# Placing a matmul stream's operands at the upper end of SBUF: the same program with other addresses

## The chip, the cores and the metric

The kernel runs on one core of one Trainium2 chip. The metric is the device time of one execution in microseconds. The kernel before was timed in three runs.

## What is computed

The reference is two transformer blocks of two layers each, on one sequence of 512 tokens with 1,024 features, all in float32. Cut to what matters here:

```python
# block 1, per layer l
h = rmsnorm(x, n1[l]) * (1 + sc1) + sh1           # sc1, sh1, g1, ... = silu(c) @ w_ada[l] + b_ada[l]
x = x + g1 * token_mixers(h, w_in[l], ...)        # conv, dilated attention, gated scan, then @ w_out[l]
h = rmsnorm(x, n2[l]) * (1 + sc2) + sh2
x = x + g2 * conv_ffn(h, w_up[l], w_down[l])      # 22 gated pairs of 128 channels
# block 2, per layer l
u = rmsnorm(x, g[l]) * (1 + scale) + shift
z = u @ w_in_2[l]                                 # three attention branches and their gates
x = x + gate * (merged(z, w_br_*) @ w_out_2[l])
```

Nearly all arithmetic is in products of a 1,024 by N weight matrix with the activations, features on partitions and tokens along the free dimension.

## The kernel before

**The weight stream.** Every weight matrix is cut into chunks of 128 output columns. A chunk is one `Slot` (line 117), and `run` (line 813) goes through the slots in order. For a slot, `w_load` brings the float32 chunk into a tile `raw` (128 by 1,024, three buffers), `w_hi` casts it to float32r in `hi`, and `w_lo` writes the remainder raw - hi to `lo` (three buffers each). The activations are held in the same form: `hh` and `hl` are the two float32r parts of the normed input, 128 partitions by 8 tiles by 512 tokens. `k_step` (line 804) then makes three matmuls per tile of 128 features, all into one PSUM bank:

```python
self.mm(p[:, c], wh, hh, start, False, cost)      # hi^T hh
self.mm(p[:, c], wh, hl, False, False, cost)      # hi^T hl
self.mm(p[:, c], wl, hh, False, stop, cost)       # lo^T hh
```

The weight part is the stationary operand, loaded before each matmul, and the activation part is the moving operand of 512 columns. At the end of a layer's half, `turn_over` (line 864) works in halves of 256 tokens, so that one half's norm runs beside the other half's products.

**Where operands lie.** Three kinds of tiles serve as operands of these products. The moving operand is `hh`/`hl`, or a piece of the arena `mx` (8 units of 512 float32r) or of the arena `rar` (24 units in the feed-forward phase, 8 in block 2), where the mixers' and the gates' results are split by `split_to`. The stationary operand is `hi`/`lo`, but in `turn_over` it can also lie in `mx` (slots marked `lead`), in `hh`/`hl` (`in_h`, line 2160) or in `rar` (`place`, line 2142).

All SBUF tiles come out of tile pools that are laid one after another from the lower end: `cst` (among others `x`, `hh`, `hl`, `mx` and the float32 arena `stay`, in this order), `ring` (`raw`, `hi`, `lo`), `adar` (`ada`), `sm`, and last a pool `work` that each phase opens anew in `phase` (line 650), with the float32 `arena`, then `rar`, then for block 2 the tables `cos` and `sin`. From the tiles' sizes, in bytes of a partition: `x` lies at 23,648, `hh` at 40,032, `hl` at 56,416, `mx` at 72,800, `stay` at 89,184, `raw` at 113,312, `hi` at 125,600, `lo` at 137,888 (to 150,176), `ada` at 150,176, `arena` from 159,136, `rar` from 175,520 in the feed-forward phase (to 224,672) and from 208,288 in block 2. The last byte used is 228,768.

**The order of the work.** The program is written out by hand: the order of each engine's instructions is fixed when the kernel is built. A planner emits stages of streams (attention, scan, norms) between the matmuls of the slots, by estimated times (`charge`, `pe`, `begin`, `keys`). Its estimates go by a tile's name and the offset inside it, not by an address. VectorE and ScalarE instructions are issued through `Timed` (line 113 in the profile), matmuls through `mm` (line 344) and transposes through `tp` (line 348); DMAs of the stream are issued on the SP queue in `load` (line 410).

Of the kernel before, what the change touches and what calls it, by code (L numbers as in the profile page):

```python
# [10 lines left out]
F32R = mybir.dt.float32r  # L11
# [6 lines left out]
P = 128  # L18
# [10 lines left out]
MIX = (0, 1, 2, 3, 4, 5, 6, 7)  # the order in which w_out takes the tiles of the mixers' results  # L29
FIRST = 4  # L30
U = 512  # one arena unit: 512 float32 per partition
# [23 lines left out]
# microseconds from the end of one engine's instruction to the start of another's that waits for it  # L55
# [3 lines left out]
# columns of the packed per-feature vectors  # L59
# [32 lines left out]
def sub(t, off, dims):  # L92
    """A view of t's partitions with its own free pattern, off elements in."""
    return bass.AP(tensor=t.tensor, offset=t.offset + off, ap=[list(t.ap[0])] + [list(d) for d in dims])


def chunked(buf):
    """A unit as [P, 4, P]."""
    return buf.ap.rearrange("p (c d) -> p c d", c=4)


class Timed:
    """An engine whose instructions also advance an estimate of when its queue is through."""
# [13 lines left out]
class Slot:  # L117
    """One product of the weight stream: psum (+)= chunk^T rhs; with parts several, of (tiles of the chunk, consume)."""
# [10 lines left out]
class Arena:  # L129
    """Memory in units. Single units come out of the smallest gaps, there the longest free one."""  # L130
# [32 lines left out]
class Arenas:  # L163
    """Working memory: a part that stays and one that a phase has."""
# [28 lines left out]
class Kernel:  # L193
    PD = 4  # weight loads this many slots ahead
    PS = 2  # splits this many slots ahead
    ARENA = 50

    def __init__(self, ctx, tc, ins, out, cfg):
# [8 lines left out]
        self.cst = pool("cst", 1)  # L207
        self.ring = pool("ring", 3)
# [20 lines left out]
    def keys(self, ap):  # L229
        """The pieces of memory an access pattern touches, as the estimate tracks them."""  # L230
        name = ap.tensor.name
        if name in self.alias:
            return (self.alias[name],)
        d = ap.ap
        lo = ap.offset % d[0][0]
        neg = sum(min(0, st * (n - 1)) for st, n in d[1:])
        pos = sum(max(0, st * (n - 1)) for st, n in d[1:])
        return [(name, u) for u in range((lo + neg) // KU, (lo + pos) // KU + 1)]

    def begin(self, eng, reads, writes):  # L240
        """When an instruction of eng may start, by what it reads and writes."""
# [73 lines left out]
    def banks(self, tag, n=2):  # L315
        """A stream's psum tiles, once those before them there are estimated to be through. Until their results
        are read, the stream must not yield."""
# [9 lines left out]
    def turned(self, pool, shape, dt, tag, bufs):  # L327
        """The next tile of a tag."""
# [34 lines left out]
    def copy(self, out, in_, scale=1.0, bias=BAL):  # L363
        """A copy on the engine that is estimated to be through with it first."""
# [45 lines left out]
    def load(self, out, src, q=None):  # L410
        """A DMA, on the SP queue unless q says another."""
# [13 lines left out]
    def drain(self, *names):  # L425
        """Emit stages until the streams of these names (none: all) are done."""
# [28 lines left out]
    def lock(self, name, n=1, room=0):  # L455
        """At most n at once; another one only with this much room."""
# [15 lines left out]
    def get(self, k=1, reserve=0):  # L472
        """Buffer for the weight stream's own results; keeps room that lets the streams go on."""
# [15 lines left out]
    def setup(self):  # L489
# [7 lines left out]
        self.hh = ct("hh", [P, KT, S], F32R)  # L497
        self.hl = ct("hl", [P, KT, S], F32R)
        self.phase_stack = self.phase_key = None
        self.mx = Arena(ct("mx", [P, 8 * U], F32R), 8)  # L500
# [26 lines left out]
    def cond(self, b):  # L527
        """silu(c) of block b on all partitions."""
# [9 lines left out]
    def start_up(self):  # L538
        """The first modulations, the input with its sums of squares and the first products, in the order in
        which DMA brings their data in."""  # L540
        b, l = self.cfg[0]
        duo = self.slots[:FIRST]
        # brings the array's clock up before the first data are in
# [106 lines left out]
    def phase(self, n, nr, rope=False):  # L650
        """New working memory: n units of float32 and nr of float32r."""
# [10 lines left out]
        self.rar = Arena(pool.tile([P, nr * U], F32R, name=self.nm("rar")), nr) if nr else None  # L662
# [5 lines left out]
    def load_consts(self):  # L668
        """A stream: the constants that are not needed at once."""
# [15 lines left out]
    def lower_bounds(self):  # L685
        """lb[l] = cumsum(p)[l] - p[0], p the softmax of lb_gamma over the layers."""
# [37 lines left out]
    def ada_until(self, b, l, t0, n):  # L724
        """The modulations t0..t0+n-1 are in and have their bias."""
# [13 lines left out]
    def w_hi(self, j):  # L739
        """The upper part of slot j's chunk, if there is room for it."""  # L740
# [8 lines left out]
        elif len(self.split) < RING:  # L749
            self.split.append(s)  # L750
            s.hi, s.lo = (self.turned(self.ring, [P, KT * P], F32R, t, RING) for t in ("hi", "lo"))
        else:
            return False
# [8 lines left out]
    def through(self, s):  # L762
        """Slot s's products are out."""
# [12 lines left out]
    def whole(self, j):  # L776
        """Whether slot j works on its chunk as it is."""
# [15 lines left out]
    def ahead(self, upto):  # L793
        """One more split, in two steps."""
# [4 lines left out]
    def until_k(self, s, p, kt, c=ALL):  # L799
        """When the products of k_step could start."""  # L800
# [41 lines left out]
    def products(self, s, c, half, *consume_at):  # L842
        """Emits a slot's products for the tokens c, with stages of the streams between them."""
# [20 lines left out]
    def turn_over(self, i, k):  # L864
        """The last k slots before a norm and the first ones after it, in halves of the tokens: one half's norm
        goes on during the other half's products."""
# [13 lines left out]
        # brings in the table of Sqrt ahead of its use  # L880
# [53 lines left out]
    def stay_get(self):  # L934
        """A unit that the change of phase leaves alone."""
# [6 lines left out]
    def go(self):  # L942
        """The next stage of a stream, whenever it comes."""
# [9 lines left out]
    def bias_mm(self, bb, duo, kt, only=None):  # L953
        """W^T B of the tile kt."""
# [5 lines left out]
    def scaled(self, accs):  # L960
        """The products of after_norm times the tokens' 1/rms."""
# [7 lines left out]
    def norm_done(self, duo, ts, bb, dve=False):  # L969
        """Shifts the scaled products of after_norm and hands them on."""  # L970
# [27 lines left out]
    def norm1_of(self, b, l):  # L998
        """Where block b's layer l has its first norm's scale, shift and weight."""
        return b, l, 8, 0, f"n1_{l}" if b == 0 else f"ng_{l}"  # L1000

    def norm_prep(self, b, l, sc, sh, w, fin):
        """Before a norm: A = weight (1 + scale), with the last norm's weight of block 1 where both follow each
        other (fin)."""
# [9 lines left out]
    def stat_tile(self, n, c=ALL):  # L1014
        """Adds the squares of x's tile n (tokens c), those of the one before it once these are on their way."""
# [16 lines left out]
    def h_raw(self, n):  # L1032
        """x's tile n times A."""
# [4 lines left out]
    def rms_rows(self, st, n, scale):  # L1038
        """1/sqrt(st*scale + eps) of st's n columns, tokens on partitions."""
# [5 lines left out]
    def norm_stream(self):  # L1045
        """rb: 1/rms of the tokens, on all partitions, from the sums of squares; with fin that of both norms,
        and rb1 that of the first."""
# [31 lines left out]
    def half_norm(self, hf, c, outs, me, after):  # L1079
        """A stream: the norm of the tokens c, as norm_stream and h_tile; with outs the last one and its result."""  # L1080
# [49 lines left out]
    def fin_stream(self):  # L1130
        """x becomes block 1's result: the last norm's weight and scale."""
# [5 lines left out]
    def h_tile(self, n, bufs, n1, n0=0):  # L1137
        """The first part of tile n and the second of tile n-1."""
# [14 lines left out]
    def v_tokens(self, vT, box):  # L1153
        """A stream: vT [feature, token] to V [token, chunk, feature]."""
# [8 lines left out]
    def two(self, outs, lhsT, rhs, start, stop, n, k0=0):  # L1163
        """The same product of n columns for both heads, side by side in the array."""
# [3 lines left out]
    def pv_add(self, pv, V, j, o, n, rhs, start, stop):  # L1168
        """pv[:, o:o+n] of both heads += V's chunk j times rhs, one operand per head."""
# [3 lines left out]
    def attend(self, heads, span, stride, size, score, V, vo, tag, done, extra=0):  # L1173
        """A stream: pv += V^T P^T of two heads, P made by score from q k^T. span(qt): the keys of query tile qt,
        from which chunk on and how many; P^T's block (kt, qt) lies at kt * stride + qt * P; score adds to the
        products itself where it takes extra units of memory."""
# [59 lines left out]
    def softmax(self, m, sc, bias, cap, nmx, rs):  # L1236
        """m = exp(sc + bias - max), of two heads; nmx: minus the maximum (that of cap too), rs: the sums."""
# [11 lines left out]
    def conv_taps(self, l, a, acc):  # L1249
        """The taps of both channel tiles, one at a time."""  # L1250
# [85 lines left out]
    def scan_stream(self, l, p, q, T0b, Kb, vbox, gbox, out):  # L1336
        """Both directions of the gated scan of heads 2p and 2p+1, by levels of sibling blocks."""
# [11 lines left out]
        def scores(w, lhsT, rhs, cost):  # L1349
            """Per chunk and block of w keys: its scores with the w queries of rhs(chunk, block), on the keys'  # L1350
            partitions."""
# [9 lines left out]
        # the scores within blocks of 32, [key, head, chunk, query of the key's block]  # L1361
# [56 lines left out]
        # between the chunks: the state after a chunk, sum over its tokens of k (decayed to its end) v  # L1418
# [72 lines left out]
    def block1_layer(self, l):  # L1491
        """Adds the layer's slots."""
# [15 lines left out]
        def give(kt):  # L1508
            """A mixer's result, to its place in w_out's order: split at once, but for the second half, which
            goes where h is until the last product with h is emitted."""  # L1510
# [808 lines left out]
```

## Time and profile before

| what | us |
|---|---|
| median of 3 runs (lowest, highest) | 2616.85 (2615.37, 2617.15) |
| span of the profiled execution, first to last instruction | 2612.9 |
| PE busy | 2567.3 (98%) |
| PEld busy (weight loads, beside PE) | 1990.7 (76%) |
| DVE busy | 1774.0 (68%) |
| ACT busy | 1339.9 (51%) |
| mean granted TensorE clock | 0.997 |

PE is the matrix engine, PEld its weight loads, DVE is VectorE, ACT ScalarE. The page's busy time of PE is a union: matmuls are pipelined and overlap one another, so a matmul's own duration is longer than the distance to the next one. What a matmul costs in a dense stream is that distance, start to start, which is read from the timeline. A row of the groups' view gives line, engine, operation, the names out<-in, partitions and columns of the array, the shape, the count, busy time and mean duration in ns, and the idle time before it.

### The profile page before, as it was taken

To read this page: it belongs to the slowest core of one execution; us is meant where nothing else is said; L and a number is where in the kernel's file an instruction comes from. 1 tells how busy PE (TensorE), PEld (TensorE's weight loads), DVE (VectorE), ACT (ScalarE), POOL (GpSimd) and SP (SyncE) were. 2 spreads that over 40 slices of the span, in tenths; PEclk is the share of its full clock that TensorE was granted. 3 is DMA by queue.
4 is the path that set the end of the run, shared out by engine and by line. 5 is a ranking of instruction groups with operands and counts; after the bars stand their busy time and mean duration, and the time that the engine had idled before them with its cause. 6 is when DMAs were issued, how large, how long until landed. Compare 5 with 4: busy or idle time off the path is not lost.

```text
span 2612.9 us, 39181 instructions
## 1 busy us (share of the span) xinstructions
PE 2567.3 (98%) x15404; PEld 1990.7 (76%) x15404; DVE 1774.0 (68%) x3368; ACT 1339.9 (51%) x2345; POOL 0.2 (0%) x4
## 2 busy tenths in 40 slices
PE   9999999999999999999999999999999999999998
PEld 5767788888977678888887677777779667777787
DVE  7898676655589767665667896556556697546645
ACT  4686553323457664342345446666435455666622
POOL 0000000000000000000000000000000000000000
PEclk9999999999999999999999999999999999999999
DMA  7433333444333232343442222223332122222222
GB/s 260 137 136 115 119 113 137 145 145 144 114 136 112 89 113 82 129 144 129 129 137 81 73 81 94 100 93 102 108 126 96 57 69 77 89 77 89 85 89 89
DMA packets 90071, 290.32 MB, mean 111 GB/s; under 512 B 10016, under 2 KB 13728, under 8 KB 89888
## 3 DMA queue, kind: packets, MB, share of 16 engines
q1 hardware_dynamic: 87728, 281.76, 31.8%
q10 hardware_dynamic: 2160, 6.06, 0.7%
q8 instruction: 122, 2.00, 0.3%
q14 instruction: 61, 0.50, 0.1%
HBM read 285.69 MB, written 2.10 MB: 110 GB/s over the span
## 4 chain that ended last, share of the span: by engine, by line
PE 85%; DVE 9%; ACT 4%; issue 1%; DMA 1%; SPq 0%; ACTq 0%; DVEq 0%
PE proj L344 70%; PE sc L344 7%; DVE arena L113 5%; PE tr L348 3%; PE pva L344 3%; ACT arena L113 2%; PE pvs L344 1%; DVE lo L113 1%; DVE sm L113 1%; ACT L113 1%; PE tr L344 1%; DVE hl L113 1%; ACT hi L113 0%; DMA arena<-w_in 0%; DMA raw<-w_in 0%
## 5 line engine op out<-in xcount | busy, mean ns | idle before, releaser
L344 PE MATMUL proj<-hh,hi 128*128 128x512 f32 (+1 forms) x2232 | 905.8, 406 | 5.7 <-ACT arena L113 3.1
L344 PE MATMUL proj<-hl,hi 128*128 128x512 f32 (+1 forms) x2232 | 879.5, 394 | 5.1 <-DVE hl L113 5.1
L344 PE MATMUL proj<-hh,lo 128*128 128x512 f32 (+1 forms) x2232 | 879.1, 394 | 0.5 <-DVE lo L113 0.5
L344 PEld LDWEIGHTS proj<-hh,hi 128*128 128x128 f32 x2232 | 419.7, 188 | 144.8 <-issue 42.5
L113 DVE TENSOR_TENSOR lo<-raw,hi 128x1024 fp32r<-128x1024 f32 (+2 forms) x381 | 436.2, 1145 | 100.8 <-ACT hi L113 95.8
L344 PEld LDWEIGHTS proj<-hh,lo 128*128 128x128 f32 x2232 | 419.8, 188 | 100.4 <-DVE lo L113 1.0
L344 PEld LDWEIGHTS proj<-hl,hi 128*128 128x128 f32 x2232 | 420.4, 188 | 95.7 <-DVE hl L113 8.3
L113 ACT CAST hi<-raw 128x1024 fp32r<-128x1024 f32 (+2 forms) x340 | 333.9, 983 | 102.9 <-PE proj L344 65.0
L344 PE MATMUL proj<-rar,hi 128*128 128x512 f32 x672 | 209.6, 393 | 0.0
L113 DVE SCALAR_TENSOR_TENSOR arena<-proj,colt,arena 128x511 f32<-128x511 f32 x164 | 122.9, 749 | 116.7 <-ACT arena L113 113.8
L113 DVE TENSOR_TENSOR arena<-arena 128x512 f32<-128x512 f32 (+8 forms) x321 | 173.0, 558 | 23.9 <-ACT arena L113 16.9
L113 ACT ACT_TABLE_LOAD x134 | 171.9, 1283 | 17.6 <-DVE sm L113 8.6
L113 ACT COPY arena<-tr 128x512 f32<-128x512 f32 (+3 forms) x266 | 111.0, 458 | 118.3 <-PE tr L348 108.2
L113 DVE SCALAR_TENSOR_TENSOR ada<-ada,cbc 128x1024 f32<-128x1024 f32 x128 | 155.8, 1217 | 0.2 <-DMA ada<-ada 0.2
L113 ACT ACTIVATE arena<-proj,colt 128x512 f32<-128x512 f32 x82 | 56.4, 688 | 184.5 <-PE proj L344 182.3
L113 ACT ACTIVATE arena<-proj 128x512 f32<-128x512 f32 x113 | 66.8, 599 | 160.2 <-PE proj L344 152.6
L344 PEld LDWEIGHTS proj<-rar,hi 128*128 128x128 f32 x672 | 124.8, 188 | 30.8 <-issue 4.6
L344 PE MATMUL sc<-arena 64*32 64x32 f32 (+6 forms) x3024 | 143.6, 248 | 3.1 <-issue 2.6
L344 PE MATMUL proj<-mx,hi 128*128 128x512 f32 x432 | 138.0, 400 | 2.4 <-DVE x L113 2.4
L113 DVE SCALAR_TENSOR_TENSOR x<-proj,mod,x 128x512 f32<-128x512 f32 (+1 forms) x102 | 64.6, 634 | 106.5 <-PE proj L344 105.7
L113 ACT ACTIVATE arena<-arena,sm 128x512 f32<-128x512 f32 (+3 forms) x180 | 105.2, 585 | 59.9 <-DVE sm L113 58.8
L344 PE MATMUL proj<-rar,lo 128*128 128x512 f32 x336 | 130.9, 390 | 0.0
(219 smaller groups left out, 3073.8 us busy)
## 6 DMA issues: line engine op xcount, KB each, us to landing
raw<-w_in SPq DMA_DIRECT2D x190, 512.0 KB, 3.3
ada<-ada SPq DMA_DIRECT2D x128, 512.0 KB, 4.5
raw<-w_up SPq DMA_DIRECT2D x88, 512.0 KB, 3.3
raw<-w_out SPq DMA_DIRECT2D x32, 512.0 KB, 3.4
raw<-w_down SPq DMA_DIRECT2D x32, 512.0 KB, 3.5
raw<-w_br SPq DMA_DIRECT2D x48, 256.0 KB, 2.7
arena<-ada SPq DMA_DIRECT2D x16, 512.0 KB, 7.3
raw<-w_down SPq DMA_DIRECT2D x16, 384.0 KB, 3.2
```

The costliest lines, as they stand in the source:

```text
L113: return f(*a, **kw)
L344: self.nc.tensor.matmul(out, lhsT, rhs, start=start, stop=stop)
L348: self.nc.tensor.transpose(out, in_, self.ident)
```

## The change

No instruction is added, removed or reordered. Tiles get other places. `hh`, `hl` and `mx` move from `cst` to a new pool `opd`, `hi` and `lo` from `ring` to a new pool `halves`, and each phase's `rar` from `work` to a pool `high` of its own. These three pools are laid on the right side, that is downwards from the upper end. What is left (`cst`, `ring` with `raw` alone, `adar`, `sm`, `work`) closes up at the lower end. The rest of the diff removes comments.

```diff
         self.cst = pool("cst", 1)
+        self.opd = pool("opd", 1, side="right")
+        self.halves = pool("halves", 3, side="right")
         self.ring = pool("ring", 3)
...
-        self.hh = ct("hh", [P, KT, S], F32R)
-        self.hl = ct("hl", [P, KT, S], F32R)
+        self.hh = self.opd.tile([P, KT, S], F32R, name="hh")
+        self.hl = self.opd.tile([P, KT, S], F32R, name="hl")
...
-        self.mx = Arena(ct("mx", [P, 8 * U], F32R), 8)
+        self.mx = Arena(self.opd.tile([P, 8 * U], F32R, name="mx"), 8)
...
-        self.rar = Arena(pool.tile([P, nr * U], F32R, name=self.nm("rar")), nr) if nr else None
+        self.rar = None
+        if nr:
+            high = self.phase_stack.enter_context(self.tc.tile_pool(name=self.nm("high"), bufs=1, side="right"))
+            self.rar = Arena(high.tile([P, nr * U], F32R, name=self.nm("rar")), nr)
...
-            s.hi, s.lo = (self.turned(self.ring, [P, KT * P], F32R, t, RING) for t in ("hi", "lo"))
+            s.hi, s.lo = (self.turned(self.halves, [P, KT * P], F32R, t, RING) for t in ("hi", "lo"))
```

## Rows read from the trace of the kernel before

**Rows 1.** The page's first part: span, busy time by engine.

```profile
span 2612.9 us, 39181 instructions
...
PE 2567.3 (98%) x15404; PEld 1990.7 (76%) x15404; DVE 1774.0 (68%) x3368; ACT 1339.9 (51%) x2345; POOL 0.2 (0%) x4
```

**Rows 2.** The chain that ended last: shares of the span by engine and line.

```profile
PE 85%; DVE 9%; ACT 4%; issue 1%; DMA 1%; SPq 0%; ACTq 0%; DVEq 0%
PE proj L344 70%; PE sc L344 7%; DVE arena L113 5%; PE tr L348 3%; PE pva L344 3%; ACT arena L113 2%; PE pvs L344 1%; DVE lo L113 1%; DVE sm L113 1%; ACT L113 1%; PE tr L344 1%; DVE hl L113 1%; ACT hi L113 0%; DMA arena<-w_in 0%; DMA raw<-w_in 0%
```

**Rows 3.** Stretches: length, PE, PEld, DVE, ACT, POOL busy, PE clock, DMA.

```profile
1050.00:1300.00 250.00, 250.00 (x1076) 201.69 (x1076) 155.38 (x199) 91.25 (x121) 0.00 (x0) 1.00 0.40 134
...
100.00:250.00 150.00, 144.18 (x1727) 103.58 (x1725) 132.72 (x277) 111.33 (x201) 0.00 (x0) 1.00 0.36 125
...
1450.00:1550.00 100.00, 95.73 (x472) 68.64 (x471) 90.68 (x187) 51.66 (x105) 0.00 (x0) 1.00 0.19 64
```

**Rows 4.** Groups by shape, PE: the stream's matmuls of 512 columns.

```profile
L344 PE MATMUL proj<-hh,hi 128*128 128x512 f32 x2200 | 896.6, 408 | 3.6 <-ACT arena L113 3.1 <-ACT hh L113 0.5
L344 PE MATMUL proj<-hl,hi 128*128 128x512 f32 x2200 | 870.6, 396 | 5.1 <-DVE hl L113 5.1
L344 PE MATMUL proj<-hh,lo 128*128 128x512 f32 x2200 | 870.2, 396 | 0.5 <-DVE lo L113 0.5
...
L344 PE MATMUL proj<-rar,hi 128*128 128x512 f32 x672 | 209.6, 393 | 0.0
...
L344 PE MATMUL proj<-mx,hi 128*128 128x512 f32 x432 | 138.0, 400 | 2.4 <-DVE x L113 2.4
L344 PE MATMUL proj<-rar,lo 128*128 128x512 f32 x336 | 130.9, 390 | 0.0
...
L344 PE MATMUL proj<-mx,lo 128*128 128x512 f32 x216 | 85.3, 395 | 0.0
```

**Rows 5.** Timeline of PE, 672.3 to 677.4 us: start, duration, what.

```profile
672.46 0.62 PE L344 MATMUL proj<-rar,hi 128*128 128x512 f32 x2
...
675.18 0.63 PE L344 MATMUL proj<-mx,hi 128*128 128x512 f32 x2
...
676.58 0.40 PE L344 MATMUL proj<-rar,hh 128*128 128x256 f32 x2
```

**Rows 6.** Timeline of PE, 313 to 317.6 us: half slots of 256 columns.

```profile
314.26 0.28 PE L344 MATMUL proj<-hl,hi 128*128 128x256 f32 x1
...
316.87 0.28 PE L344 MATMUL proj<-hh 128*128 128x256 f32 x1
...
317.59 0.28 PE L344 MATMUL proj<-hh 128*128 128x256 f32 x1
```

**Rows 7.** Groups by shape, PE: matmuls of 256 columns, by where the weights lie.

```profile
L344 PE MATMUL sc<-hh,mx 128*128 128x256 f32 x224 | 53.6, 284 | 0.0
...
L344 PE MATMUL proj<-hl,rar 128*128 128x256 f32 x64 | 17.7, 277 | 0.0
...
L344 PE MATMUL proj<-mx,hl 128*128 128x256 f32 x16 | 4.5, 284 | 0.0
```

**Rows 8.** Groups by shape, DVE: one operation on high and on low tiles.

```profile
L113 DVE TENSOR_TENSOR arena<-arena 128x512 f32<-128x512 f32 x159 | 109.2, 688 | 9.7 <-ACT arena L113 6.0 <-PE sc L344 2.1
...
L113 DVE TENSOR_TENSOR sq<-sq,arena 128x512 f32<-128x512 f32 x32 | 21.5, 684 | 0.1
```

**Rows 9.** Groups by shape, ACT: one operation into high and into low tiles.

```profile
L113 ACT COPY arena<-tr 128x512 f32<-128x512 f32 x107 | 60.0, 589 | 48.3 <-PE tr L348 38.8 <-PE tr L344 6.0 <-ACT hi L113 1.9
...
L113 ACT COPY stay<-tr 128x512 f32<-128x512 f32 x8 | 4.7, 585 | 3.7 <-PE tr L348 3.7
```

**Rows 10.** Groups by shape, PE: transposes out of high and of low tiles.

```profile
L348 PE MATMUL tr<-ident,arena 128*128 128x128 f32 x742 | 111.9, 274 | 11.4 <-DVE arena L113 5.9 <-ACT arena L113 5.2
...
L348 PE MATMUL tr<-ident,stay 128*128 128x128 f32 x78 | 11.7, 274 | 0.0
```

**Rows 11.** Waits of PE: total us, times, longest.

```profile
PE tr L348 <- DVE arena L113: 5.9, 8, 1.0
```

## The prediction

> **What bounds the kernel now.** I read the page first. PE is busy for 98% of the span, DVE for 68%, ACT for 51% [rows 1]. The chain of waits agrees: 85% of it runs through PE, and 70% of the span through the matmuls into `proj`, the weight stream; DVE holds 9% and ACT 4% [rows 2]. The stretches show two kinds of time. From 1050 to 1300 us PE never idles and does nothing but the stream, 1,076 matmuls in 250 us, 232.3 ns each, while DVE works 62% of the time. In the attention and scan stretches DVE is nearly full: 132.7 of 150 us from 100 on, 90.7 of 100 us from 1450 on [rows 3]. So a shorter matmul pays in full in the first kind and in part in the second.
>
> **What a stream matmul costs.** Its duration (about 395 ns, [rows 4]) overlaps the next one's, so I take start-to-start distances. The piece of timeline at 672 us is the heart of the argument. It lies inside one slot of w_down: the same weight tiles, the same PSUM bank, only the moving operand goes from `rar` to `mx`. From the first `rar` row shown to the `mx` row stand 12 matmuls in 675.18 - 672.46 = 2.72 us, **226.7 ns** each; from there to the last row, 6 matmuls on `mx` in 1.40 us, **233.3 ns** each [rows 5]. The granted clock is 1.00, the 2.4 GHz level, and 512 columns are 213.3 ns at it. So `rar` pays 13 ns over the columns and `mx` 20. `rar` lies at 175,520 bytes and above, `mx` at 72,800; `hh` and `hl`, below `mx`, go with `mx` (the 232.3 ns of the pure stretch is their mixture with some `rar`). Neither DVE nor ACT work explains the step, since it comes at the tile's change.
>
> Weights have their own step. At 256 columns, 23 matmuls from 314.26 to 316.87 us with weights in `hi`/`lo` (125,600 and above) come every 113.5 ns; the next six, weights in `hh`/`hl` (40,032 and above), every 0.72 / 6 = 120.0 ns, moving operand low in both [rows 6]. Durations say the same: 284 ns with weights in `mx` or `hl`, 277 ns with weights in `rar` [rows 7].
>
> **The change part by part.** Taking the old top of 228,768 for the upper end, `hh`, `hl`, `mx` now fill about 180 to 229 thousand bytes, `hi`/`lo` 155 to 180 thousand, and `rar` what lies below: 106 to 155 thousand in the feed-forward phase, 139 to 155 in block 2.
> 1. *Moving operands `hh`, `hl`, `mx` go up.* 2,200 x 3 + 432 + 216 = 7,248 matmuls of 512 columns [rows 4], from 233.3 to 226.7 ns: 7,248 x 6.6 = 47.8 us of PE time. How much of it is on the path? All stream matmuls into `proj` take about 8,256 x 232.6 ns plus 912 half ones at 0.118 us, 2,028 us; the chain holds 70.2% of 2612.9 = 1,834 us of them, 0.90 [rows 2]. So **-43.0 us**; bounds: 0, if height is not the cause, and -47.8.
> 2. *Weights that lay in `mx`, `hh`, `hl` go up.* Eleven groups of 256 columns, 960 matmuls (largest and smallest in [rows 7]), 120.0 to 113.5 ns: 6.2 us, x 0.90 = **-5.6 us**.
> 3. *`hi`/`lo` rise from 126-150 to 156-180 thousand.* On `rar` they already allow 226.7 ns, and at 256 columns 113.5. I take **0**; bounds: -25 us, half a step of 6.6 ns on 8,256 matmuls x 0.90, and 0.
> 4. *`rar` sinks.* In the feed-forward phase 2 x 8 slots x 18 tiles x 3 = 864 of its 1,008 matmuls [rows 4] read from 106 to 155 thousand bytes, where no moving operand lay before. The nearest rows are slow at 89 thousand and below [rows 5] and, for weights, fast from 126 thousand on [rows 6]. Two thirds of the region is in the latter, so I take **+1 us**; bounds 0 and 864 x 6.6 ns x 0.90 = +5.1.
> 5. *Everything else sinks* (`arena`, `stay`, `raw`, `ada`). The tensor-tensor operation takes 688 ns on `arena` (high) and 684 into `sq` (low) [rows 8], the copy out of PSUM 589 into `arena` and 585 into `stay` [rows 9], a transpose 274 ns from either [rows 10]. These cost **0**. The DMAs and their issues are the same; only the destinations move. With four changes of phase the new `arena` and `rar` overlay old working memory as before; the cover is the queue of stream matmuls ahead, and one late stage costs about what PE's longest total wait shows per time, 5.9 us in 8 times [rows 11], so 3 us at most.
> 6. *What is late next.* With PE 2.8% quicker in the stream, DVE and ACT have that much less time for the same work. In the full stretches (about 450 us of the kind of 100 to 250 and 1450 to 1550 [rows 3]) a third to a half of PE's time is stream, worth some 6 us; I take half of that as lost to DVE and ACT stages that come late, **+3 us**.
>
> Sum: -43.0 - 5.6 + 0 + 1 + 0 + 3 = -44.6 us. The span of the profiled execution becomes 2612.9 - 44.6 = 2568.3; the median of the runs lies 3.95 above that span, so 2616.85 - 44.6, about **2572 us** (-1.7%). From the bounds: all of parts 1 and 2 on the path, no loss elsewhere, 2616.85 - 54 = 2563; with half a step from part 3 about 2548.
>
> **A rule against this.** The step between `rar` and `mx` at 672 us is 6.6 ns per matmul [rows 5], and by it the sum is -44.6 us. The Trainium skill, page "SBUF — State Buffer", section "Who interferes with whom", says that the matrix engine has two read ports of its own and never waits on anyone, and the page "TensorE: Matmul & The Clock Gate" (section "Wait — 56ns, not 53.3ns?") gives a back-to-back distance that depends on the columns alone, 215.7 ns at 512. By that a tile's place has no price and the sum would be 0. The 226.7 and 233.3 ns, both above 215.7 and different in one slot, speak against it.
>
> **The rivals.**
> - *No change (12%).* What differs at 672 us is not the height but something that goes with it, and that the new places don't mend. For it: `rar` is slow in no row and low in none, so height and everything else of that tile go together. Against it: weights in `hi`/`lo`, at another height and in another pool, show a step of the same size [rows 6]. Time: 2617. It is also what the page's rule above gives.
> - *A further step (9%).* The tile's start inside a line counts, not its height: before, all operands start at odd multiples of 32 bytes, afterwards (sizes are multiples of 2,048, counted from the top) at even places. `rar`'s own 13 ns over the columns [rows 5] would then shrink by another 6.6 ns: 8,256 x 6.6 ns x 0.90 = 49 us more, 2523.
> - *Half of it (9%).* The stream gets its 226.7 ns, but DVE and ACT take back half in the stretches where they are full [rows 3] and at the halves of `turn_over`, or only one of the two operands gains: 2616.85 - 22 = 2595.
> - *Slower (11%).* The two reads of PE disturb each other when both operands lie in the same part of SBUF. For it: the slow 256-column rows have both low, and the quick ones (weights in `hi`/`lo` or `rar`, moving operand low) have them apart [rows 6, 7]; the quick `rar` matmuls have weights 25 thousand bytes or more away. Now both lie above 155 thousand everywhere. Price: another step of 6.6 ns on all 8,256, to 240 ns, and `rar` from 226.7 to 240: 8,256 x 6.6 x 0.90 + 1,008 x 6.6 x 0.90 = 55 us, 2672. It decides from the point where the pure stretch shows more than 233.3 ns per matmul. Against it: `mx` with `hi`/`lo` 40 thousand bytes away is slow, `rar` at about the same distance above them is quick [rows 5].
>
> **How the numbers follow.** The forecast has 59%, the rivals 12, 9, 9 and 11. A measurement of this kernel tells about 0.2%, 5 us, from no change. Faster: 59 + 9 + 9 = 77%; same: 12%; slower: 11%. The forecast's own range is 2560 to 2590. The range goes down to 2548, the bound with half a step from the weights, and up to 2618, which takes in the half case and no change; it leaves out the further step and the slower case, 20%.
>
> **What would show it.** In the profile of the changed kernel: the pure stretch (now around 1,030 us into the span) at 226 to 228 ns per matmul, from the count of a stretch of 250 us, about 1,100 instead of 1,076; durations of `proj<-hl,hi` at about 389 instead of 394 ns; all 256-column groups at 276 to 278 ns; `rar` unchanged, or towards 233 ns if its new place is low. DVE and ACT groups keep their means. PE's waits on DVE and ACT grow by a few us. The prediction is wrong if the pure stretch stays at 232 ns (no change), goes above 233.3 (the two reads collide) or falls to 220 (start, not height).

## The result, and the profile after

The changed kernel takes 2586.65 us (median of 4 runs, 2585.22 to 2588.26) against 2616.75 us of the kernel before in the same comparison (4 runs, 2615.37 to 2617.15): a ratio of **0.9886, 95% interval 0.9872 to 0.99**, 30 us faster. The forecast was 2572 us. The profiled execution of the changed kernel took 2588.26 us, its span is 2586.5 us, 26.4 us less than before [rows 1]. This execution is the slowest of the four, with a mean granted clock of 0.995 where the others have 0.997; where that shows in the trace is said below.

The first two views answer to [rows 1, 2]: the page's busy times, and its chain that ended last. Lines of code have moved by two: L346 is the matmul, L350 the transpose.

```profile
span 2586.5 us, 39181 instructions
...
PE 2538.2 (98%) x15404; PEld 1995.5 (77%) x15404; DVE 1773.5 (69%) x3368; ACT 1339.2 (52%) x2345; POOL 0.2 (0%) x4
...
PE 82%; DVE 10%; ACT 4%; DMA 2%; issue 1%; SPq 0%; ACTq 0%; DVEq 0%
PE proj L346 68%; PE sc L346 7%; DVE arena L113 6%; PE tr L350 3%; PE pva L346 3%; ACT arena L113 3%; DVE lo L113 1%; PE pvs L346 1%; ACT L113 1%; DVE sm L113 1%; PE tr L346 1%; DVE hl L113 1%; DVE ada L113 0%; ACT hi L113 0%; DMA arena<-w_in 0%
```

The same 15,404 matmuls take 29.1 us less of PE; DVE and ACT have the same work to 0.7 us. PE is still the bound, its share of the chain down from 85 to 82%.

The stretches, as in [rows 3] (length, busy time of PE, PEld, DVE, ACT and POOL with instruction counts, granted clock, DMA share, GB/s):

```profile
1050.00:1300.00 250.00, 249.74 (x1103) 206.54 (x1102) 154.47 (x198) 89.31 (x118) 0.00 (x0) 1.00 0.41 134
100.00:250.00 150.00, 144.07 (x1724) 103.81 (x1722) 132.51 (x276) 110.86 (x201) 0.00 (x0) 0.99 0.35 125
1450.00:1550.00 100.00, 95.04 (x472) 71.42 (x473) 94.33 (x201) 47.45 (x93) 0.00 (x0) 1.00 0.24 80
```

The pure stretch holds 1,103 matmuls instead of 1,076: 250 / 1,103 = **226.7 ns** each instead of 232.3. (The count takes in the matmuls that run across the stretch's two edges, so such a quotient can be off by 0.3 ns; start to start the stretch has 232.5 ns before, and 226.7 after but for one wait of PE.) In the stretch from 100 us, where DVE is busy 132.5 of 150 us, hardly anything has moved: 1,724 matmuls against 1,727. The stream's groups by shape (instructions, busy us, mean ns of one, idle before), to lay beside [rows 4, 7, 10]:

```profile
L346 PE MATMUL proj<-hl,hi 128*128 128x512 f32 x2200 | 860.6, 391 | 5.3 <-DVE hl L113 5.3
...
L346 PE MATMUL proj<-rar,hi 128*128 128x512 f32 x672 | 208.9, 392 | 0.0
...
L350 PE MATMUL tr<-ident,arena 128*128 128x128 f32 x742 | 113.2, 276 | 12.7 <-DVE arena L113 9.7 <-ACT arena L113 2.9
...
L346 PE MATMUL proj<-mx,lo 128*128 128x512 f32 x216 | 84.3, 390 | 0.0
...
L346 PE MATMUL sc<-hh,mx 128*128 128x256 f32 x224 | 53.8, 285 | 0.0
...
L346 PE MATMUL proj<-hl,rar 128*128 128x256 f32 x64 | 18.1, 283 | 0.0
```

The 512-column groups on `hl` and `mx` fall by 5 ns and now equal those on `rar`, which has sunk by 69,000 bytes without harm. But the half slots have not gained: `proj<-hl,rar` rises from 277 to 283 ns. The timeline of PE (start, duration) at the place of [rows 5] shows both:

```profile
664.09 0.61 PE L346 MATMUL proj<-rar,hi 128*128 128x512 f32 x2
...
667.49 0.61 PE L346 MATMUL proj<-mx,hi 128*128 128x512 f32 x2
...
668.85 0.40 PE L346 MATMUL proj<-rar,hh 128*128 128x256 f32 x2
...
676.76 0.40 PE L346 MATMUL proj<-rar,hh 128*128 128x256 f32 x2
```

From the first row to the second stand 15 matmuls on `rar` in 3.40 us, then 6 on `mx` in 1.36 us: 226.7 ns on both, so the step of [rows 5] is gone. After them 66 half products in 7.91 us, 119.8 ns each. Two rows of PE's waits, to [rows 11] (total us, times, longest):

```profile
PE tr L350 <- DVE arena L113: 9.7, 12, 1.1
...
PE proj L346 <- DVE arena L113: 2.6, 2, 2.3
```

**The account.** I added up the start-to-start distances of all PE rows in both traces, by what the row is: 2603.8 us before, 2577.3 after. Stream products of 512 columns on `hh`, `hl`, `mx`: those followed within 250 ns, some 6,750, went from 233.3 to 228.1 ns, -35.1 us; those that a wait or another kind of work follows, +2.9. On `rar`: -0.7. Half slots: 117.9 to 119.9 ns, +2.6. Transposes: 126.9 to 130.3 ns, 820 of them, +2.7. All else +1.2. Together -26.4 us.

**The clock in this trace.** In two stretches of 3.4 us each the granted clock is 0.5, the 1.2 GHz level: from 163.0 us, one microsecond behind a wait of PE of 2.30 us, and from 886.6 us, at the end of a wait of 1.64 us. In the timeline of PE (the number in brackets is the wait before):

```profile
162.01 0.50 PE L346 MATMUL proj<-hh,hi 128*128 128x512 f32 x1 [2.30 <-DVE arena L113]
...
164.47 2.08 PE L346 MATMUL sc<-arena,stay 64*128 64x512 f32 x4
...
886.85 0.90 PE L350 MATMUL tr<-ident,arena 128*128 128x128 f32 x3 [1.64 <-ACT arena L113]
...
888.40 0.63 PE L346 MATMUL proj<-hh,lo 128*128 128x512 f32 x1
888.83 0.63 PE L346 MATMUL proj<-hh,hi 128*128 128x512 f32 x1
```

In the kernel before the same four score matmuls take 1.13 us, and its clock is 1.00 at both places. The distances that begin in the two stretches are 3.1 us longer than the same ones before, and they stand in the account: 1.2 us in the +2.9, 0.9 in the transposes, 0.9 in all else. What makes the clock fall there is not shown: the kernel before has the wait of 1.64 us too and keeps its clock, and of the runs below low_192 has both stretches, high_192 neither, and sweep_a, slower than the kernel before, the first.

### The profile page after: what moved, and what is told of

The parts are those of the page before. It is cut to its first block, busy times and chain, and to the rows that moved or that the text cites. A ratio compares the mean times of both kernels' runs of the same rounds, so it can differ in the third digit from the quotient of the medians.

```text
span 2586.5 us, 39181 instructions
## 1 busy us (share of the span) xinstructions
PE 2538.2 (98%) x15404; PEld 1995.5 (77%) x15404; DVE 1773.5 (69%) x3368; ACT 1339.2 (52%) x2345; POOL 0.2 (0%) x4
## 4 chain that ended last, share of the span: by engine, by line
PE 82%; DVE 10%; ACT 4%; DMA 2%; issue 1%; SPq 0%; ACTq 0%; DVEq 0%
PE proj L346 68%; PE sc L346 7%; DVE arena L113 6%; PE tr L350 3%; PE pva L346 3%; ACT arena L113 3%; DVE lo L113 1%; PE pvs L346 1%; ACT L113 1%; DVE sm L113 1%; PE tr L346 1%; DVE hl L113 1%; DVE ada L113 0%; ACT hi L113 0%; DMA arena<-w_in 0%
## 5 line engine op out<-in xcount | busy, mean ns | idle before, releaser
L346 PE MATMUL proj<-hh,hi 128*128 128x512 f32 (+1 forms) x2232 | 896.9, 402 | 7.0 <-DVE arena L113 2.6
L346 PE MATMUL proj<-hl,hi 128*128 128x512 f32 (+1 forms) x2232 | 869.7, 390 | 5.3 <-DVE hl L113 5.3
L346 PE MATMUL proj<-hh,lo 128*128 128x512 f32 (+1 forms) x2232 | 869.8, 390 | 0.5 <-DVE lo L113 0.5
L346 PEld LDWEIGHTS proj<-hh,hi 128*128 128x128 f32 x2232 | 420.2, 188 | 138.3 <-issue 43.9
L346 PEld LDWEIGHTS proj<-hh,lo 128*128 128x128 f32 x2232 | 419.9, 188 | 90.3 <-DVE lo L113 1.0
L346 PEld LDWEIGHTS proj<-hl,hi 128*128 128x128 f32 x2232 | 420.7, 188 | 85.4 <-DVE hl L113 8.5
L346 PE MATMUL proj<-rar,hi 128*128 128x512 f32 x672 | 208.9, 392 | 0.0
L346 PEld LDWEIGHTS proj<-rar,hi 128*128 128x128 f32 x672 | 124.9, 188 | 29.7 <-issue 4.6
L346 PE MATMUL sc<-arena 64*32 64x32 f32 (+6 forms) x3024 | 143.8, 248 | 3.5 <-issue 3.1
L346 PE MATMUL proj<-mx,hi 128*128 128x512 f32 x432 | 136.3, 397 | 2.5 <-DVE x L113 2.5
L346 PE MATMUL proj<-rar,lo 128*128 128x512 f32 x336 | 130.9, 390 | 0.0
```

The source lines that it names most:

```text
L346: self.nc.tensor.matmul(out, lhsT, rhs, start=start, stop=stop)
```

## The experiments

The half slots do not fit height: where weights and moving operand both rose (`proj<-hl,hi` of 256 columns, 277 to 283 ns), those products got slower too. So I looked at the addresses again. Modulo 256 bytes, `hh`, `hl`, `mx` started at 96 before and `hi`, `lo`, `rar` at 160; the float32r sizes are multiples of 2,048, so every slice keeps its tile's remainder. In the changed kernel (`hh` 180,192; `hl` 196,576; `mx` 212,960; `hi` from 155,616; `lo` from 167,904; `rar` 106,464 and 139,232) all remainders are 224. By this reading, **the start of the weights less the start of the moving operand, modulo 256 bytes** (the offset, from here on) decides, and height doesn't. The quick `rar` matmuls of [rows 5] had offset 0 (175,520 - 125,600 = 195 x 256), the slow `mx` ones 64 (125,600 - 72,800 = 206 x 256 + 64). That 195 is odd, and the distance of `hi` to `hh` in the changed kernel even (96 x 256), shows that no larger power of two than 256 counts.

**low_192.** The kernel before, with everything low as it was, and one unused tile behind the constants, which moves what lies behind them (`raw`, `hi`, `lo`, `ada`, `arena`, `rar`) up by 192 bytes and so makes the offset 0:

```diff
         self.A1 = ct("A1", [P, 8])
+        self.pad = ct("pad", [P, 48])
```

> The kernel before with 192 unused bytes behind its constants: hi, lo, arena and rar start 192 bytes higher, so that hi and lo now start at the same place modulo 256 as hh, hl and mx (all at 96), while all of them stay in the lower part of SBUF as before. Theory A, height (the forecast): hh, hl and mx are still low, so the pure stretch stays at 232 to 233 ns per 512-column matmul and the time near 2617 us. Theory B, relative start: what counts is where the weights start against the moving operand modulo 256; the changed kernel has them equal by its new layout, so this one gets 226.7 to 228 ns on hh, hl, mx and rar as well, all half slots of 256 columns about 120 ns, and a time near 2587 us.

Measured: 2586.8 us beside 2615.59 of the kernel before on the same chip. The pure stretch:

```profile
1050.00:1300.00 250.00, 250.00 (x1104) 206.93 (x1104) 154.98 (x200) 90.06 (x120) 0.00 (x0) 1.00 0.41 136
```

1,104 matmuls, 226.7 ns each start to start, with no operand at the upper end. The half slots stand at 119.8 ns, 119.9 in the changed kernel, as theory B says.

**high_192.** The reverse: the changed kernel, with 192 bytes between the operands `hh`, `hl`, `mx` and the weights, all still at the upper end. The offset is 64 again, as before.

```diff
         self.opd = pool("opd", 1, side="right")
+        self.padp = pool("padp", 1, side="right")
+        self.pad = self.padp.tile([P, 48], F32, name="pad")
         self.halves = pool("halves", 3, side="right")
```

> The changed kernel with 192 unused bytes between the pool of hh, hl, mx and the pool of hi, lo: everything stays at the upper end, but hi, lo (and rar below them) start 64 bytes further modulo 256 than hh, hl and mx, as in the kernel before. Theory A, height: nothing changes, 226.7 to 228 ns per matmul and about 2587 us. Theory B, relative start: the matmuls on hh, hl and mx go back to 233.3 ns, those on rar stay at 226.7, half slots with weights in hi and lo come every 113.5 ns, and the time is 2610 to 2617 us.

Measured: 2614.68 us beside 2615.59; the span is 2612.9, that of the kernel before to the tenth. The pure stretch:

```profile
1050.00:1300.00 250.00, 250.00 (x1077) 201.70 (x1076) 155.35 (x199) 91.21 (x121) 0.00 (x0) 1.00 0.40 134
```

Of its groups by shape, a plain one of the stream:

```profile
L348 PE MATMUL proj<-hl,hi 128*128 128x512 f32 x2200 | 871.3, 396 | 6.3 <-DVE hl L113 6.1
```

1,077 matmuls and 396 ns: the height is kept and the gain is gone. The two runs together settle it: 192 bytes are worth 28 us, and 140,000 bytes of height (`hh` at 40,032 here, at 180,192 there) nothing that shows.

**low_192_timed.** The same kernel as low_192, timed, to see whether height adds anything.

> The kernel before with 192 bytes of padding, once more and timed. If the relative start is the whole of the change, this kernel is as fast as the changed one: a ratio to the kernel before of 0.987 to 0.990. If the height adds something of its own, it lies measurably outside that: below 0.985 or above 0.992.

Measured: 2587.07 us (2584.85 to 2588.22, 4 runs), ratio 0.9887, interval 0.987 to 0.9903. It cannot be told from the changed kernel (0.9886). The medians lie 0.4 us apart, and each interval reaches some 4 us to either side. So the rest of the change, the height of the operands and the new places of the working memory, the raw weights and the modulations, is in sum worth nothing that these runs can tell.

**sweep_a, sweep_b, sweep_c.** The changed kernel, with the three buffers each of `hi` and `lo` at three different offsets in turn; `hh`, `hl`, `mx` and `rar` keep equal remainders. The edit takes each buffer as a tile of its own with a lead of some elements:

```diff
+LEADS = {"hi": [(8, 1032), (16, 1040), (8, 1032)], "lo": [(40, 1064), (16, 1040), (8, 1064)]}
...
-            s.hi, s.lo = (self.turned(self.halves, [P, KT * P], F32R, t, RING) for t in ("hi", "lo"))
+            s.hi, s.lo = (self.phased(t) for t in ("hi", "lo"))
...
+        lead, width = LEADS[tag][i]
+        t = self.halves.tile([P, width], F32R, tag=f"{tag}{i}", name=self.nm(tag), bufs=1)
...
+        return t[:, lead:lead + KT * P]
```

> The changed kernel with the three buffers of hi (and of lo) starting 32, 96 and 128 bytes further modulo 256 than hh, hl and mx, so that every third slot of the stream has the same relation. Theory A, height: all slots at 226.7 to 228 ns. Theory B, relative start: the slots differ, in a pattern of three; 0 bytes is known as 226.7 and 64 as 233.3; 128 should be near 226.7 if the relation counts modulo 128, else it is open; 32 and 96 are open, between 216 and 240 ns. Time 2570 to 2625 us.

> As sweep_a with 160, 192 and 224 bytes. Theory A, height: all slots at 226.7 to 228 ns. Theory B, relative start: 192 is 233.3 if the relation counts modulo 128 (as 64), else open; 160 and 224 are open and, modulo 128, the same as 32 and 96. Time 2570 to 2625 us.

> The changed kernel, with the three buffers of hi and lo starting 240, 48 and 16 bytes behind a multiple of 256 from the moving operand. If what counts is which 64-byte piece of 256 each operand is in, a shift of 16 bytes either way costs part of the step: 226.7 to 231 ns per matmul of 512 columns at 16 and 240, 233.3 at 48, and a time between 2595 and 2612 us. If only the exact equality counts (the same place in the line of both), all three are at 233.3 ns and the time is 2612 to 2624. If there is a better place than equality, one of the three shows 220 ns.

Measured: 2623.08 us (offsets 32, 96, 128), 2616.93 us (160, 192, 224) and 2599.1 us (16, 48, 240), beside 2615.59, 2615.59 and 2615.8 of the kernel before. Each sweep shows its offsets side by side, since the slots take the buffers in turn, 24 matmuls a slot. In the timeline of PE in sweep_c, the first rows of four slots:

```profile
1060.31 0.40 PE L359 MATMUL proj<-hh,hi 128*128 128x512 f32 x1
...
1065.90 0.39 PE L359 MATMUL proj<-hh,hi 128*128 128x512 f32 x1
...
1071.35 0.39 PE L359 MATMUL proj<-hh,hi 128*128 128x512 f32 x1
...
1076.79 0.40 PE L359 MATMUL proj<-hh,hi 128*128 128x512 f32 x1
```

5.59 us for the slot at offset 48, 5.45 at 240 and 5.44 at 16; over 24, **232.9, 227.1 and 226.7 ns**. Two-decimal starts leave 0.4 ns of doubt in each. The same in sweep_b, for 160, 192 and 224:

```profile
1047.00 0.39 PE L359 MATMUL proj<-hh,hi 128*128 128x512 f32 x1
...
1052.60 0.40 PE L359 MATMUL proj<-hh,hi 128*128 128x512 f32 x1
...
1058.11 0.40 PE L359 MATMUL proj<-hh,hi 128*128 128x512 f32 x1
...
1063.71 0.39 PE L359 MATMUL proj<-hh,hi 128*128 128x512 f32 x1
```

233.3, 229.6 and 233.3 ns. The means over all consecutive 512-column products (start to start, under 260 ns) of a whole trace:

| offset, bytes | ns | products | run |
|---|---|---|---|
| 0 | 227.8 | 7,581 | after |
| 16 | 228.9 | 2,402 | sweep_c |
| 32 | 233.2 | 2,404 | sweep_a |
| 48 | 233.2 | 2,477 | sweep_c |
| 64 | 233.3 | 6,575 | before |
| 96 | 234.1 | 2,479 | sweep_a |
| 128 | 232.8 | 2,388 | sweep_a |
| 160 | 233.5 | 2,403 | sweep_b |
| 192 | 229.5 | 2,474 | sweep_b |
| 224 | 233.3 | 2,388 | sweep_b |
| 240 | 227.6 | 2,389 | sweep_c |

Offset 0 is good with 16 bytes to spare on either side, 192 is half good, everything else that was tried costs 5 to 6 ns a product against offset 0. sweep_c came out as the first of its three outcomes. No offset tried reached 220 ns. That 128 is slow and 0 quick shows that the pattern doesn't repeat at 128; that 64 and 192 differ shows that it depends on which operand is ahead.

**pairs.** Does it depend on the start alone, or on how the two reads walk through memory? In the changed kernel `hi` and `lo` share one tile, element by element by turns, so that a weight load steps over 8 bytes per element; the three tiles have `hi` at offsets 0, 64 and 128.

```diff
+        t = self.halves.tile([P, width], F32R, tag=f"pair{i}", name=self.nm("pair"), bufs=1)
...
+        v = t[:, lead:lead + 2 * KT * P].rearrange("p (n two) -> p two n", two=2)
+        return v[:, 0], v[:, 1]
```

> The changed kernel, with hi and lo of a weight tile element by element by turns in one tile, so that a weight load strides over 8 bytes for each element and covers twice the bytes; the three tiles start 0, 64 and 128 bytes behind a multiple of 256 from the moving operand. If the loss comes from a load and a stream that walk through the 256 bytes at different speeds and meet, the starts that are best now need not be: one of the three starts should give a new spacing, 220 ns at best, and others 233.3 or more. If a weight load with stride is itself slower or reads more lines, all three starts show 233.3 to 240 ns and the time is 2615 to 2660 us; splits on VectorE and ScalarE that write with a stride may add waits on top.

Measured: 2619.2 us beside 2615.8. The pure stretch:

```profile
1050.00:1300.00 250.00, 250.00 (x1081) 209.81 (x1080) 157.47 (x202) 94.88 (x121) 0.00 (x0) 1.00 0.39 133
```

The groups by shape that the stride touches:

```profile
L362 PEld LDWEIGHTS proj<-hl,pair 128*128 128x128 f32 x2232 | 436.1, 195 | 82.8 <-DVE hl L114 11.9
...
L114 DVE TENSOR_TENSOR pair<-raw,pair 128x1024 fp32r<-128x1024 f32 x321 | 392.2, 1222 | 40.2 <-ACT pair L114 38.7
...
L114 ACT CAST pair<-raw 128x1024 fp32r<-128x1024 f32 x285 | 321.7, 1129 | 77.0 <-PE proj L362 55.8 <-issue 14.5 <-DMA raw<-w_out 4.3
```

By tile, start to start within it: 233.2 to 233.6 ns at 0, 230.3 at 64, 231.3 to 231.8 at 128 (some 2,400 products each). So offset 0, best with packed weights, is worst with strided ones: the walk counts, not the start as such. Neither of the two expected outcomes came out whole: there is a new best start, but at 230, not 220 ns, and no start is slower than 234. The load takes 195 ns instead of 188 in the changed kernel, ACT's cast 1129 instead of 1044; DVE's subtraction is unharmed (1222, 1220 in the changed kernel).

**lo_64.** Which matmul pays, the one whose weights are at a bad offset or the one beside whose stream they are loaded? `hi` at offset 0, `lo` at 64:

```diff
+LEADS = {"hi": [(0, 1024), (0, 1024), (0, 1024)], "lo": [(16, 1040), (0, 1024), (0, 1072)]}
```

> The changed kernel, with hi where it is (equal start, modulo 256 bytes, with the moving operand) and lo 64 bytes further on. The order within a slot is hh by hi, hl by hi, hh by lo, over and over. If a matmul is held up by the load of the next one's weights, the matmul ahead of each lo product is the slow one: proj<-hl,hi at 396 to 398 ns and proj<-hh,lo at 391 as in the changed kernel. If it is its own weights that count, it is the other way round: proj<-hh,lo slow and proj<-hl,hi at 391. In both cases the pure stretch from 1050 to 1300 us holds about 1092 matmuls (a mean of 228.9 ns, two fast and one slow), and the time lies a third of the way back, about 2596 us. If both count, two of three are slow: 1081 matmuls, 2606 us.

Measured: 2608.39 us beside 2617.69. The pure stretch:

```profile
1050.00:1300.00 250.00, 250.00 (x1083) 203.20 (x1083) 156.29 (x200) 90.91 (x121) 0.00 (x0) 1.00 0.39 134
```

Two of its groups by shape:

```profile
L359 PE MATMUL proj<-hh,lo 128*128 128x512 f32 x2200 | 873.5, 397 | 0.5 <-DVE lo L114 0.5
L359 PE MATMUL proj<-hl,hi 128*128 128x512 f32 x2200 | 865.1, 393 | 4.9 <-DVE hl L114 4.8
```

1,083 matmuls, 231.1 ns each start to start: three products take 693.3 ns, 13.3 more than three at 226.7. One weight load in three at a bad offset costs twice what it costs in a stream where all are (6.6 ns each). By the time that is the third outcome named, but no product is as quick as 226.7: from the start of the `lo` product to the next start pass 235.8 ns, from that of `hh` by `hi` 228.3 and from that of `hl` by `hi`, beside which the `lo` weights are loaded, 229.2. The durations too put most of it on the `lo` product (397), a little on the one ahead (393 against 391). Inconclusive as to which read waits, since the row's start and end are not the start of its reads; clear as to the use: `hi` and `lo` have to agree.

## Why the prediction was right or wrong

- **Part 1, moving operands.** The effect was there, the cause named for it was not. The step that failed is the reading of 672 us as height ("`rar` lies at 175,520 bytes and above, `mx` at 72,800"). The two tiles also differed in offset, 0 and 64; low_192 and high_192 show that the offset alone makes the step. The new places happen to have offset 0, since everything at the upper end is stacked in multiples of 2,048 bytes from one edge. So -43.0 us was forecast, by a wrong route, and -35.1 came, beside +2.9 for the products that a wait or another kind of work follows. That the forecast has the right direction is luck: with 192 bytes between the two pools the same rise is worth nothing (high_192).
- **Its size.** The forecast took 226.7 ns for all 7,248 products and 0.90 of them as path. Where PE does nothing but the stream, that is what came. Elsewhere the stream has to settle: after scores or transposes the first products of a run are still slow. The timeline of PE in the changed kernel, behind four score matmuls:

```profile
151.58 0.39 PE L346 MATMUL proj<-hl,hi 128*128 128x512 f32 x1
...
153.43 0.39 PE L346 MATMUL proj<-hh,hi 128*128 128x512 f32 x1
153.66 0.39 PE L346 MATMUL proj<-hl,hi 128*128 128x512 f32 x1
...
157.97 0.39 PE L346 MATMUL proj<-hh,lo 128*128 128x512 f32 x1
```

  8 products in 1.85 us (231 ns), then 19 in 4.31 us (226.8 ns). Over the whole trace some 330 runs of the stream begin so: the first three products at 232 to 233 ns, the next four at 229 to 231, the next three at 227.5 to 229, from the eleventh on 226.7; in the kernel before, 232 to 233.7 at every place. Summed over these places the excess is 8.6 us, nearly all of what is missing between 6,750 x 6.6 = 44.6 us and 35.1. (The row's 394 ns, from which the prediction counts `proj<-hl,hi` down by 5, is 396 in [rows 4]; the fall to 391 is as forecast.)
- **Part 2, half slots: wrong sign.** -5.6 us forecast, +2.6 came. In [rows 6] the quick 113.5 ns had offset 64 (weights in `hi`, moving operand in `hh`) and the slow 120.0 offset 0 (`hh` and `hl` both). At 256 columns offset 0 is a bad one, 119.9 ns over 1,590 products of the changed kernel, and the change gives offset 0 to all of them. The forecast was too large as well: 288 of its 960 products, those with `rar` as moving operand, stood at 118 ns and not at 120. And the trace before had rows against height that the prediction passed over: half slots into `pva` and `sc` with weights in `hi`/`lo` last 281 to 286 ns, as long as those with low weights in [rows 7]. The step that failed is that of part 1 again: two rows that differ in height and in offset, put down to height.
- **Part 3, 0 us, and part 4, +1 us.** As far as height goes right: `hi`/`lo` and `rar` lost nothing, `rar` even 0.8 ns per product. The bound of -25 us for a further step in the weights didn't come, in any of the offsets tried.
- **Part 5, everything else 0.** Right as far as the runs show. With `arena` at 85,408 bytes now, its tensor-tensor operation and the copy out of PSUM take what they took in [rows 8, 9] (688 and 589 ns). That is the better evidence: the row into `sq` that stood for low tiles reads `arena` too. The groups by shape say:

```profile
L113 DVE TENSOR_TENSOR arena<-arena 128x512 f32<-128x512 f32 x159 | 109.2, 687 | 10.8 <-ACT arena L113 7.2 <-PE sc L346 2.0
...
L113 ACT COPY arena<-tr 128x512 f32<-128x512 f32 x107 | 60.0, 589 | 47.7 <-PE tr L350 38.2 <-PE tr L346 6.0 <-ACT hi L113 1.8
```

  The transposes take 276 instead of 274 ns [rows 10], +2.7 us by their distances, but not for their place: in high_192, where `arena` lies at the very bytes of the changed kernel, they are back at 126.9 ns. 2.6 of the 2.7 us lie in distances of more than 250 ns, where PE waits or the clock is low, so they belong to part 6.
- **Part 6, late stages, +3 us.** About right for the waits: PE's idle time before its instructions grew from 38.2 to 40.8 us in all. Transposes wait for DVE 9.7 instead of 5.9 us [rows 11] and for ACT 2.9 instead of 5.2, and where PE waits 2.3 us for DVE in the stream it waited 2.0 us for ACT before. What the forecast has no term for is the clock: the two stretches at 1.2 GHz cost 3.1 us on top, in this trace.
- **The rivals.** *No change* had the right doubt, that "something that goes with it" and not the height makes the step, and was wrong only in that the new places do mend it. *Slower* named a mechanism that would fit, the two reads of PE disturbing each other, but not when: what costs time is not operands in one part of SBUF but bad offsets, and sweep_a is slower than the kernel before (2623.08 against 2615.59 us). *A further step* looked at the tile's start, but of each tile by itself, and its premise wasn't met: the new places lie at 224 modulo 256, again an odd multiple of 32. No offset tried went below 226.7 ns. *Half of it* is nearer in time (2595) than the forecast (2572), though not by the engines that it blamed; "only one of the two operands gains" describes part 1 without part 2.
- **The rule weighed there.** 192 bytes of padding change the time by 28 us with the same instructions. The Trainium skill, page "SBUF — State Buffer", section "Who interferes with whom", gives PE two independent read ports and has it never wait on anyone. That the place of a tile has no price, as the rule was read there, is contradicted. Whether PE's two reads disturb each other is not shown: the measured 226.7 and 233.3 ns, at either height, go with the distance of their two operands, which independent ports do not explain for these float32r streams whose weights are loaded anew for every product. That PE waits on another engine here is not shown by any run either.

What stays open is the mechanism below the offset. At the lower clock nothing is lost. The granted clock of the kernel before is 0.5, the 1.2 GHz level, from 43.4 us, in the midst of a row of 40 products of one column, to 53.6, and there the stream runs at offset 64:

```profile
49.52 0.63 PE L344 MATMUL proj<-hl,hi 128*128 128x512 f32 x1
...
52.93 0.63 PE L344 MATMUL proj<-hh,hi 128*128 128x512 f32 x1
```

Eight products in 3.41 us, 426 to 427 ns each, which is one column per cycle and nothing on top. By the same count 512 columns are 213.3 ns at 2.4 GHz. 6.67 ns is the time of 16 columns there, or 64 bytes of the moving operand in each partition, and 512 columns take 213.3 ns and two such steps at offset 0, three at most others; half slots take 106.7 ns and one or two. Means between these (229 at 192, 230 in pairs) say that not every product loses the same. This fits a stream and a load that walk over four pieces of 64 bytes and now and then want the same one, and it fits the settling, since a lost step changes their distance in time. It is only argued: no run observes the memory.

I did not try to give the half slots an offset of their own. Their weights lie in three kinds of tile that also serve as moving operands. At 113.5 instead of 119.9 ns for all 1,590 of them it would be 10 us at most, and offset 64 alone doesn't give that: in the kernel before, 658 half products at this offset have a mean of 116.4 ns; many of them stand between products at offset 0.

## What to carry to other kernels

For float32r matmuls with a weight load each, work out the start of the weights less the start of the moving operand modulo 256 bytes first: here 0 (within 16 bytes) was best for 512 columns and bad for 256, and `hi` and `lo` had to agree. One unused tile of 192 bytes did as much as rebuilding the layout. And where two rows of a profile differ in one property, list what else of them differs, the low bits of the address too, before the property gets the credit.

## What the runs showed of the hardware that was not expected

- The distance between two float32r products of 512 columns depends on the offset modulo 256 bytes: 226.7 ns steady at 0, about 229.5 at 192, 233 to 234 at all others tried outside 16 bytes around 0, at a granted clock of 1.00.
- Offset 0 takes full effect only some ten products after an interruption (231 ns, then 226.7).
- At a granted clock of 0.5 the step is gone: 427 ns for 512 columns at offset 64 too.
- One bad load in three costs 13.3 ns per three products, three in three cost 20.
- A weight load with a step of 8 bytes takes 195 instead of 188 ns in its row and turns the order of the offsets round (233 ns at 0, 230 at 64).
